# Turning matmuls that use half of TensorE's array, and moving transfers between queues, in a two-layer hybrid decoder trunk

## The chip, the cores and the metric

The kernel runs on one core of one Trainium2 chip. The metric is the device time of one execution in microseconds (us). The core has five engines that run beside each other: TensorE (PE; its weight loads are the row PEld), VectorE (DVE), ScalarE (ACT), GpSimd (POOL) and SyncE (SP), which here only issues transfers.

## The reference

Two decoder layers over 256 tokens of width 1024, all float32. Each layer projects the tokens, runs three mixers on parts of the projection, gates and sums them, and ends in a SwiGLU network. Cut to what matters here:

```python
for l in range(DEPTH):
    p = x @ w_in[l]
    y_a = rwkv7_time_mix(p[..., :o_mla], ...)      # 8 heads of 64, recurrence over the tokens
    y_b = mla_branch(p[..., o_mla:o_s5], ...)      # 8 heads, softmax(q k) v, causal
    y_c = s5_branch(p[..., o_s5:o_gate], ...)      # 32 groups, diagonal complex state space
    gates = sigmoid(p[..., o_gate:] + gate_b[l])
    merged = gates[0] * y_a + gates[1] * y_b + gates[2] * y_c
    x = layer_norm(ALPHA * x + merged @ w_out[l], ln1_g[l], ln1_b[l])
    h = silu(x @ ffn_w1[l]) * (x @ ffn_w3[l])
    x = layer_norm(ALPHA * x + h @ ffn_w2[l], ln2_g[l], ln2_b[l])
```

The RWKV step is `state = state * w + (state a) b + v k`, `y = state r`, one 64x64 state per head.

## The kernel before

**Weights.** All large weights come as 138 chunks per layer, 128x1024 float32 (0.5 MB; four of a layer have 832 columns). `w_load` (L156) issues the transfer into `raw` on SP (L160), ACT rounds it to `whi` (L161), and DVE, with POOL's help at times, forms the rest `wlo` (L171, L173). There are three `raw` buffers and four pairs `whi`/`wlo`; `w_next` keeps up to four chunks ahead. A projection (`mm3`, L206 to L208) is three matmuls per block: high by high, high by low, low by high. These projections are most of PE's work.

**Order.** The mixers are written as short pieces, and two tables of tokens, `ORDER1` and `ORDER2` (one row per layer), say in which order the pieces are issued: `S`, `m`, `r` and `G` are projections (S5 input, latents, RWKV input, gates), `P` loads the small parameters, `T` makes the S5 tables, `t` is an S5 tile, `N` the latents' norm; in the second table `p`, `s`, `i`, `v`, `n` are the RWKV pieces `prep`, `scores`, `inverse`, `solve` and `norm`, `a` and `b` the two halves of `attn`, and `l`, `o`, `h`, `f` projections of outputs and gates. A scheduler then sets each engine's order from these pieces, the pools' buffers and its own estimates. Each engine runs its list strictly in that order.

**Small products.** Many products use only part of the 128x128 array: 64 rows, or 64 columns, or a quarter. A plain float32 matmul is two passes (two records each in the profile). The ones that the change touches:
- `s5_tile` (L726): eight products with 64 rows each, four on the lower half of the partitions, then four on the upper.
- `prep` (L867, L871): the two lora products, rows 0 to 63 and 64 to 127; L921 transposes v; L891 and L916 are other transposes.
- `scores` (L940): four products of head 0 (lower rows), then four of head 1 (upper rows), into two banks.
- `solve` (L1031 to L1070): the recurrence for a pair `g` of head blocks (`e` = 0, 1, each two heads) in four steps `b` of 64 tokens. In a step, L1031 and L1035 form the right side, it is copied to `RH` (tile Gc) by ACT, L1043 multiplies by the inverse, DVE copies the result into `ST`, L1053 and L1055 form the new state, and two DVE operations (L1059) scale it into `S0`. Both head blocks lie on the same half `rb` of the partitions. At the end L1067 and L1070 form the outputs of all four steps.
- `attn` (L1217 to L1221): per call, two heads `hg` and `hg + 4`; each is transposed, copied to `PT` (two buffers) and multiplied by v. An even `hg` writes columns 0 to 63 of the array, an odd one 64 to 127, of one bank that is held from the even call to the odd one.

**Transfers besides weights.** `token_major` (L498) is the output projection and the second FFN product, with the layer norm. It loads `lg`, `lb` (0.5 MB each) and `xk` (1 MB) at the chunk `at`: 2 of 8 and 12 of 22. All on SP. `U2`, the S5 input in another layout, comes by eight small transfers (L695), also on SP. POOL makes the next layer's S5 tables beside layer 0's FFN (last operations L384 to L389) in buffers that are freed when it is done and that `lg`, `lb` and `xk` of the second product then take.

## Time and profile before

| | us |
|---|---|
| median of three runs | 1076.62 (1067.44, 1076.62, 1078.77) |
| profiled execution | 1068.97 |
| its span, first to last instruction | 1067.1 |
| PE, DVE, ACT, POOL busy | 1014.2, 784.7, 482.6, 235.2 |

The mean granted TensorE clock is 0.986 of 2.4 GHz. Busy time of PE is the union of its matmuls; a matmul's length includes the end of its pipeline, some 0.2 us in which the next one already runs. So in a timeline the distance from start to start tells what a matmul costs, not its length. The chain that ended last is 58% PE, 17% DVE, 9% POOL and 7% DMA.

### The profile page before, as it was taken

The page shows a single profiled execution, that of the slowest core. Times are in us where ns is not written, and L with a number is a line of the kernel's source. Part 1 is how long each engine was busy: PE and PEld are TensorE (multiplying, and loading weights), DVE is VectorE, ACT ScalarE, POOL GpSimd, SP SyncE. Part 2 cuts the span into 40 slices and gives each one's busy share as a digit, 9 for nine tenths or more (in the row PEclk, how much of TensorE's full clock was granted, in tenths as well). Part 3 has the DMA queues.
Part 4 walks back from the last instruction along what each step waited for, and adds up shares of the span by engine and source line. Part 5 has one row for each costly group of instructions (what it writes and reads, how often), then busy time and mean ns, then how long its engine had stood idle before and what let it go on. Part 6 is the DMA issues. An engine that isn't in the chain of part 4 may idle for free.

```text
span 1067.1 us, 21219 instructions
## 1 busy us (share of the span) xinstructions
PE 1014.2 (95%) x8560; PEld 912.5 (86%) x8560; DVE 784.7 (74%) x1542; ACT 482.6 (45%) x797; POOL 235.2 (22%) x262
## 2 busy tenths in 40 slices
PE   8799989999999999799999999999999999999997
PEld 7798778888896999798878999778889879999885
DVE  7969978976578778386474998888747876667546
ACT  5544477534244244144325346865334423443431
POOL 2970222300000599500012003221002420000000
PEclk9989999999999999999999999999999999999999
DMA  8442241223385555466536325232234755555562
GB/s 280 156 159 90 91 147 41 92 89 100 93 294 177 197 180 171 162 207 217 185 123 218 126 81 191 79 98 85 76 100 173 252 190 215 183 188 183 179 196 79
DMA packets 47394, 163.86 MB, mean 154 GB/s; under 512 B 5696, under 2 KB 8256, under 8 KB 46400
## 3 DMA queue, kind: packets, MB, share of 16 engines
q1 hardware_dynamic: 47008, 161.98, 45.9%
q8 instruction: 67, 1.10, 0.4%
q10 hardware_dynamic: 288, 0.52, 0.1%
q14 instruction: 31, 0.25, 0.1%
HBM read 156.72 MB, written 4.19 MB: 151 GB/s over the span
## 4 chain that ended last, share of the span: by engine, by line
PE 58%; DVE 17%; POOL 9%; DMA 7%; ACT 5%; issue 3%; SPq 0%; DVEq 0%; ACTq 0%; POOLq 0%
PE mm L208 11%; PE mm L207 10%; PE mm L206 10%; DMA raw<-in_ws 6%; DVE wlo L171 3%; PE mm L511 3%; PE mm L512 3%; PE mm L510 3%; ACT whi L161 3%; DVE z L745 1%; PE pa L726 1%; PE pb L1035 1%; POOL st L387 1%; PE pb L1043 1%; PE pa L940 1%
## 5 line engine op out<-in xcount | busy, mean ns | idle before, releaser
L171 DVE TENSOR_TENSOR wlo<-raw,whi 128x1024 fp32r<-128x1024 f32 (+2 forms) x265 | 333.5, 1262 | 171.8 <-ACT whi L161 169.1
L161 ACT CAST whi<-raw 128x1024 fp32r<-128x1024 f32 (+2 forms) x267 | 277.4, 1043 | 379.8 <-PE mm L207 211.8
L206 PE MATMUL mm<-xh,whi 128*128 128x256 f32 x1312 | 376.9, 287 | 14.2 <-ACT whi L161 13.9
L208 PE MATMUL mm<-xh,wlo 128*128 128x256 f32 x1312 | 376.1, 287 | 2.9 <-DVE wlo L171 2.6
L207 PE MATMUL mm<-xl,whi 128*128 128x256 f32 x1312 | 375.1, 286 | 0.4 <-DVE xl L262 0.4
L206 PEld LDWEIGHTS mm<-xh,whi 128*128 128x128 f32 x1312 | 249.2, 190 | 18.6 <-ACT whi L161 14.5
L208 PEld LDWEIGHTS mm<-xh,wlo 128*128 128x128 f32 x1312 | 250.2, 191 | 7.6 <-DVE wlo L171 4.0
L207 PEld LDWEIGHTS mm<-xl,whi 128*128 128x128 f32 x1312 | 250.2, 191 | 2.7 <-DVE xl L262 0.6
L240 POOL TENSOR_TENSOR rs<-rs,mhalf 128x1 f32<-128x1 f32 x8 | 7.8, 971 | 341.2 <-DVE rs L238 341.2
L206 PE MATMUL mm<-yh,whi 128*128 128x256 f32 x256 | 74.6, 291 | 0.1
L207 PE MATMUL mm<-yl,whi 128*128 128x256 f32 x256 | 74.1, 289 | 0.0
L208 PE MATMUL mm<-yh,wlo 128*128 128x256 f32 x256 | 74.1, 289 | 0.0
L511 PE MATMUL mm<-wlo,hh 128*128 128x512 f32 x132 | 52.0, 394 | 0.0
L510 PE MATMUL mm<-whi,hh 128*128 128x512 f32 x132 | 51.7, 394 | 0.0
L512 PE MATMUL mm<-whi,hl 128*128 128x512 f32 x132 | 51.5, 392 | 0.0
L206 PEld LDWEIGHTS mm<-yh,whi 128*128 128x128 f32 x256 | 48.5, 189 | 2.3 <-ACT qa L113 0.9
L207 PEld LDWEIGHTS mm<-yl,whi 128*128 128x128 f32 x256 | 48.5, 190 | 1.2 <-issue 0.8
L208 PEld LDWEIGHTS mm<-yh,wlo 128*128 128x128 f32 x256 | 48.6, 190 | 1.1 <-issue 0.7
L240 POOL TENSOR_TENSOR rsn<-rsn,mhalf 128x8 f32<-128x8 f32 x4 | 6.5, 1634 | 142.8 <-DVE rsn L238 142.8
L173 POOL TENSOR_TENSOR wlo<-raw,whi 128x384 fp32r<-128x384 f32 (+2 forms) x24 | 27.7, 1162 | 44.6 <-ACT whi L161 42.5
L947 POOL TENSOR_SCALAR_AFFINE_SELECT Mk<-Mk 64x512 f32<-64x512 f32 x32 | 27.0, 844 | 43.6 <-ACT Mk L113 42.3
L510 PEld LDWEIGHTS mm<-whi,hh 128*128 128x128 f32 x132 | 24.8, 188 | 6.2 <-DVE th L1284 0.8
(487 smaller groups left out, 1745.7 us busy)
## 6 DMA issues: line engine op xcount, KB each, us to landing
raw<-in_ws SPq DMA_DIRECT2D x267, 512.0 KB, 3.8
raw<-in_ws SPq DMA_DIRECT2D x8, 416.0 KB, 3.5
xd<-xk SPq DMA_DIRECT2D x3, 1024.0 KB, 4.1
xk<-xd SPq DMA_DIRECT2D x3, 1024.0 KB, 7.4
lg<-in_lnv SPq DMA_DIRECT2D x4, 512.0 KB, 5.0
lb<-in_lnv SPq DMA_DIRECT2D x4, 512.0 KB, 5.7
pc<-in_spC SPq DMA_DIRECT2D x2, 768.0 KB, 5.3
pb<-in_spB SPq DMA_DIRECT2D x2, 512.0 KB, 4.9
```

The lines of the kernel that those rows point to most:

```text
L161: S.copy(out=hi[:, s], in_=raw[:, s])
L171: V.tensor_tensor(out=lo[:, 0:m], in0=raw[:, 0:m], in1=hi[:, 0:m].bitcast(F32), op=ALU.subtract)
L173: G.tensor_tensor(out=lo[:, m:w], in0=raw[:, m:w], in1=hi[:, m:w].bitcast(F32), op=ALU.subtract)
L206: PE.matmul(ps, lhsT=wh, rhs=xh, start=first, stop=False)
L207: PE.matmul(ps, lhsT=wh, rhs=xl, start=False, stop=False)
L208: PE.matmul(ps, lhsT=wl, rhs=xh, start=False, stop=last)
L240: G.tensor_tensor(out=out, in0=in_, in1=mh(out), op=ALU.pow)
L387: E.tensor_tensor(out=s1, in0=c0, in1=ls, op=ALU.mult)
L510: PE.matmul(acc[b][n], lhsT=ah, rhs=w[0][:, s], start=(k == 0), stop=False)
L511: PE.matmul(acc[b][n], lhsT=ah, rhs=w[1][:, s], start=False, stop=False)
L512: PE.matmul(acc[b][n], lhsT=al, rhs=w[0][:, s], start=False, stop=(k == nk - 1))
L947: G.affine_select(out=Mk[r, h], in_=Mk[r, h], pattern=[[0, 4], [1, 2], [1, 64]], compare_op=ALU.is_ge, fill=0.0, base=-1, channel_multipli ...
```

## The change

- A helper `in_turn` issues matmuls in a fixed sequence. With it the S5 input products, the lora products and the scores alternate between the lower and upper row half, and take both banks at once.
- `solve` is mirrored: the head block `e` = 1 now has its time halves swapped (`rb` is a list, one slice per head block), so that in each step the two blocks lie on opposite halves. Products of both alternate. `RH` is one copy of 128x128 instead of 64x256 on ACT; `ST` is copied by ACT for `e` = 0 and DVE for `e` = 1. The output block alternates over the steps' halves.
- For that, odd blocks in `prep` write B and K in swapped places (one more DVE operation), transpose v by two-pass products into the swapped column halves, and two index expressions in `inverse` are mirrored (not shown).
- `attn` keeps `PT` of an even call (three buffers) and multiplies in the odd call, alternating the column halves; its bank is held only there.
- `U2` is loaded from ACT's queue instead of SP's.
- `token_major` issues its loads, `xk` in two halves, spread over the chunks in the list `at`, each behind the last weight transfer issued.
- In layer 1's first table `r0` moves ahead of `N t0`.

```diff
-    "m S0 S1 P N t0 r0 r1 r2 t1 r3 w0 w1 t2 t3 g0 r4 r5 w2 w3 G3 G1 G2 r6 G0 g1",
+    "m S0 S1 P r0 N t0 r1 r2 t1 r3 w0 w1 t2 t3 g0 r4 r5 w2 w3 G3 G1 G2 r6 G0 g1",
...
-            SY.dma_start(out=raw[:, s], in_=ws[i, :, s])
+            state["dma"] = SY.dma_start(out=raw[:, s], in_=ws[i, :, s])
...
+    def in_turn(mms):
...
+        last = None
+        for ps, lhsT, rhs in mms:
+            with tc.issue_after(inst(last)) if last is not None else ExitStack():
+                last = PE.matmul(ps, lhsT=lhsT, rhs=rhs, start=True, stop=True)
...
+        loads = [(xk[:, 0], x_dram[:, 0]), (lg, lnv[l, ln:ln + 1, :].to_broadcast([128, D])),
+                 (lb, lnv[l, ln + 1:ln + 2, :].to_broadcast([128, D])), (xk[:, 1], x_dram[:, 1])]
...
-            if k == at:
-                SY.dma_start(out=lg, in_=lnv[l, ln:ln + 1, :].to_broadcast([128, D]))
-                SY.dma_start(out=lb, in_=lnv[l, ln + 1:ln + 2, :].to_broadcast([128, D]))
-                SY.dma_start(out=xk, in_=x_dram)
...
+            if k in at:
...
+                with tc.issue_after(inst(state["dma"])):
+                    for o, i in loads[at.index(k)::len(at)]:
+                        SY.dma_start(out=o, in_=i)
...
-                        SY.dma_start(out=U2[r:r + 32, j // 2::2, :], in_=u[32 * j:32 * j + 32, :, i, :])
+                        S.dma_start(out=U2[r:r + 32, j // 2::2, :], in_=u[32 * j:32 * j + 32, :, i, :])
...
+                pss = [mxps("a"), mxps("a")]
+                in_turn([(pss[pp][:, 256 * qq + 128 * ri:256 * qq + 128 * ri + 128],
+                          bl[64 * pp:64 * pp + 64, 2 * F + qq, ri, :], U2[64 * pp:64 * pp + 64, 2 * F + qq, :])
+                         for qq in range(2) for ri in range(2) for pp in range(2)])
...
-                    ps = mxps("a")
-                    for qq in range(2):
-                        for ri in range(2):
-                            PE.matmul(ps[:, 256 * qq + 128 * ri:256 * qq + 128 * ri + 128],
-                                      lhsT=bl[64 * pp:64 * pp + 64, 2 * F + qq, ri, :],
-                                      rhs=U2[64 * pp:64 * pp + 64, 2 * F + qq, :], start=True, stop=True)
-                    ps4 = ps.rearrange("p (q r t) -> p q r t", q=2, r=2)
+                    ps4 = pss[pp].rearrange("p (q r t) -> p q r t", q=2, r=2)
...
-                ps = mxps("a")
-                PE.matmul(ps[:, 0:256], lhsT=w2a2[0:64, 128 * f:128 * f + 128], rhs=ld[0:64], start=True, stop=True)
+                pss = [mxps("a"), mxps("a")]
+                in_turn([(pss[i][:, 0:256], w2a2[64 * i:64 * i + 64, 128 * f:128 * f + 128], ld[64 * i:64 * i + 64])
+                         for i in range(2)])
...
-                S.activation(out=uu, in_=ps[:, 0:256], func=AF.Tanh, bias=hw0[:, f:f + 1], scale=0.5)
-                ps = mxps("a")
-                PE.matmul(ps[:, 0:256], lhsT=w2a2[64:128, 128 * f:128 * f + 128], rhs=ld[64:128], start=True, stop=True)
+                S.activation(out=uu, in_=pss[0][:, 0:256], func=AF.Tanh, bias=hw0[:, f:f + 1], scale=0.5)
...
-                S.activation(out=ta, in_=ps[:, 0:256], func=AF.Tanh, bias=ha0[:, f:f + 1], scale=0.5)
+                S.activation(out=ta, in_=pss[1][:, 0:256], func=AF.Tanh, bias=ha0[:, f:f + 1], scale=0.5)
...
-                    PE.transpose(ps[:, 128 * b:128 * b + 128], vT[:, f, 128 * b:128 * b + 128], ident)
+                    if e:
+                        for i in range(2):
+                            o = 128 * b + 64 * i
+                            PE.matmul(ps[64 - 64 * i:128 - 64 * i, 128 * b:128 * b + 128], lhsT=vT[:, f, o:o + 64], rhs=ident,
+                                      start=True, stop=True, skip_group_check=True)
+                    else:
+                        PE.transpose(ps[:, 128 * b:128 * b + 128], vT[:, f, 128 * b:128 * b + 128], ident)
...
-                    r = slice(64 * i, 64 * i + 64)
+                    r = slice(64 * (i ^ e), 64 * (i ^ e) + 64)
...
+                pss = [mxps("a"), mxps("a")]
+                in_turn([(pss[h][:, 128 * b:128 * b + 128],
+                          BK[64 * h:64 * h + 64, b // 2, 2 * (b % 2):2 * (b % 2) + 2].rearrange("p a t -> p (a t)"),
+                          AR[64 * h:64 * h + 64, :, b]) for b in range(4) for h in range(2)])
...
-                    o = slice(64 * h, 64 * h + 64)
-                    ps = mxps("a")
-                    for b in range(4):
-                        PE.matmul(ps[:, 128 * b:128 * b + 128],
-                                  lhsT=BK[o, b // 2, 2 * (b % 2):2 * (b % 2) + 2].rearrange("p a t -> p (a t)"),
-                                  rhs=AR[o, :, b], start=True, stop=True)
-                    cp(9, out=Mk[:, h].rearrange("p b a t -> p (b a t)"), in_=ps)
+                    cp(9, out=Mk[:, h].rearrange("p b a t -> p (b a t)"), in_=pss[h])
...
-                    rb, rk = slice(64 - 64 * i, 128 - 64 * i), slice(64 * i, 64 * i + 64)
+                    rb = [slice(64 * (1 - i ^ e), 64 * (1 - i ^ e) + 64) for e in range(2)]
+                    rk = rb[::-1]
...
+                    if b:
+                        for e in range(2):
+                            PE.matmul(ps[rb[e], 0:128], lhsT=ARs[e][:, 0, b, :], rhs=S0[:, e, b - 1], start=True,
+                                      stop=False, skip_group_check=True)
+                    for h in range(2):
+                        o = slice(64 * h, 64 * h + 64)
+                        for e in range(2):
+                            PE.matmul(ps[rb[e], o], lhsT=Mks[e][rk[e], h, b, 0, :], rhs=ST[rk[e], e, c2, i, h, :],
+                                      start=(b == 0), stop=True, skip_group_check=True)
+                    RH = t1("Gc", (128, 4, 65))[:, 0:2, 0:64]
+                    cp(16, out=RH, in_=v2(ps[:, 0:128], 2))
+                    ps = mxps("b")
+                    for h in range(2):
+                        for e in range(2):
+                            PE.matmul(ps[rb[e], 64 * h:64 * h + 64], lhsT=DTf[rb[e], 4 * e + 2 * h + c2, :],
+                                      rhs=RH[rb[e], h, :], start=True, stop=True, skip_group_check=True)
...
-                        if b:
-                            PE.matmul(ps[rb, 128 * e:128 * e + 128], lhsT=ARs[e][:, 0, b, :], rhs=S0[:, e, b - 1], start=True,
-                                      stop=False, skip_group_check=True)
-                        for h in range(2):
-                            o = 128 * e + 64 * h
-                            PE.matmul(ps[rb, o:o + 64], lhsT=Mks[e][rk, h, b, 0, :], rhs=ST[rk, e, c2, i, h, :],
-                                      start=(b == 0), stop=True, skip_group_check=True)
-                    RH = t1("Gc", (128, 4, 65))[:, :, 0:64]
-                    cp(16, out=RH[rb], in_=v2(ps[rb, 0:256], 4))
-                    ps = mxps("b")
-                    for e in range(2):
-                        for h in range(2):
-                            o = 128 * e + 64 * h
-                            PE.matmul(ps[rb, o:o + 64], lhsT=DTf[rb, 4 * e + 2 * h + c2, :], rhs=RH[rb, 2 * e + h, :],
-                                      start=True, stop=True, skip_group_check=True)
-                    cp(17, out=ST[rb, :, c2, i], in_=ps[rb, 0:256].rearrange("p (e h v) -> p e h v", e=2, h=2))
+                        cp(16 + e, out=ST[rb[e], e, c2, i], in_=v2(ps[rb[e], 0:128], 2))
...
-                    for b in range(4):
-                        r, o = slice(64 * (b % 2), 64 * (b % 2) + 64), 256 * (b // 2) + 128 * e
-                        if b:
-                            PE.matmul(ps[r, o:o + 128], lhsT=ARs[e][:, 1, b, :], rhs=S0[:, e, b - 1], start=True, stop=False,
-                                      skip_group_check=True)
+                    for c2 in range(2):
...
+                                r = slice(64 * (b % 2), 64 * (b % 2) + 64)
+                                PE.matmul(ps[r, o:o + 128], lhsT=ARs[e][:, 1, b, :], rhs=S0[:, e, b - 1], start=True,
+                                          stop=False, skip_group_check=True)
...
-                            PE.matmul(ps[r, o + 64 * h:o + 64 * h + 64], lhsT=Mks[e][:, h, b, 1, :],
-                                      rhs=ST[:, e, b // 2, b % 2, h, :], start=(b == 0), stop=True, skip_group_check=True)
+                            for b in bs:
+                                r = slice(64 * (b % 2), 64 * (b % 2) + 64)
+                                PE.matmul(ps[r, o + 64 * h:o + 64 * h + 64], lhsT=Mks[e][:, h, b, 1, :],
+                                          rhs=ST[:, e, c2, b % 2, h, :], start=(b == 0), stop=True, skip_group_check=True)
...
-                    acc_o[0] = mxps("c")
-                po = acc_o[0]
-                o = 64 * (hg % 2)
+                    acc_o[0] = []
+                else:
+                    po = mxps("c")
...
-                    PT = mqs[0].tile([128, 384], F32, tag="PT", name="PT", bufs=2)
+                    PT = mqs[0].tile([128, 384], F32, tag="PT", name="PT", bufs=3)
...
-                    PE.matmul(po[o:o + 64, 256 * i:256 * i + 256], lhsT=vt[:, 0, 64 * h:64 * h + 64], rhs=PT[:, 0:256],
-                              start=True, stop=False, skip_group_check=True)
-                    PE.matmul(po[o:o + 64, 256 * i + 128:256 * i + 256], lhsT=vt[:, 1, 64 * h:64 * h + 64],
-                              rhs=PT[:, 256:384], start=False, stop=True, skip_group_check=True)
-                if hg % 2 == 1:
-                    cp(26, out=yB[0][:, hg // 2::2], in_=v2(po, 2))
-                    V.tensor_tensor(out=yB[1][:, hg // 2::2], in0=v2(po, 2),
-                                    in1=yB[0][:, hg // 2::2].bitcast(F32), op=ALU.subtract)
+                    if hg % 2 == 0:
+                        acc_o[0].append((PT, h, 0))
+                        continue
...
+                    two = acc_o[0][i], (PT, h, 64)
+                    for p, h, o in two:
+                        PE.matmul(po[o:o + 64, 256 * i:256 * i + 256], lhsT=vt[:, 0, 64 * h:64 * h + 64], rhs=p[:, 0:256],
+                                  start=True, stop=False, skip_group_check=True)
+                    for p, h, o in two:
+                        PE.matmul(po[o:o + 64, 256 * i + 128:256 * i + 256], lhsT=vt[:, 1, 64 * h:64 * h + 64],
+                                  rhs=p[:, 256:384], start=False, stop=True, skip_group_check=True)
+                if hg % 2 == 0:
+                    yield
+                    return
+                cp(26, out=yB[0][:, hg // 2::2], in_=v2(po, 2))
+                V.tensor_tensor(out=yB[1][:, hg // 2::2], in0=v2(po, 2),
+                                in1=yB[0][:, hg // 2::2].bitcast(F32), op=ALU.subtract)
...
-            token_major(gate0[1], 8, 0, False, q, l, 2)
+            token_major(gate0[1], 8, 0, False, q, l, [0, 1])
...
-                token_major((hh, hl), NF, 2, l == layers - 1, q2, l, 12)
+                token_major((hh, hl), NF, 2, l == layers - 1, q2, l, [9, 10, 11, 12])
```

The scheduler's result, at three places. On PE, in layer 0's first pair, step 3 of the recurrence before (S is `S0`, Gc is `RH`, c the identity; `mm` rows are projections):

```order
L207 MATMUL mm<-xl,whi 128x256
L208 MATMUL mm<-xh,wlo 128x256
L1031 MATMUL pb<-S_1666,kr__236 64x128
L1035 MATMUL pb<-ST,Mk 64x64 x2
L1031 MATMUL pb<-S_1666,kr__236 64x128
L1035 MATMUL pb<-ST,Mk 64x64 x2
L206 MATMUL mm<-xh,whi 128x256
L207 MATMUL mm<-xl,whi 128x256
L208 MATMUL mm<-xh,wlo 128x256
L206 MATMUL mm<-xh,whi 128x256
L1043 MATMUL pb<-Gc,DTf_1662 64x64 x4
L1053 MATMUL pb<-S_1666,c 64x64
```

The same and the next step after the change, with line numbers moved by some 10 to 30:

```order
L1051 MATMUL pb<-S_1666,kr__236 64x128 x2
L1056 MATMUL pb<-ST,Mk 64x64 x4
L1063 MATMUL pb<-Gc,DTf_1662 64x64 x4
L1074 MATMUL pb<-S_1666,c 64x64
L1076 MATMUL pb<-ST,BKt 64x64
L1074 MATMUL pb<-S_1666,c 64x64
L1076 MATMUL pb<-ST,BKt 64x64
L1074 MATMUL pb<-S_1666,c 64x64
L1076 MATMUL pb<-ST,BKt 64x64
L1074 MATMUL pb<-S_1666,c 64x64
L1076 MATMUL pb<-ST,BKt 64x64
L1051 MATMUL pb<-S_1666,kr__236 64x128 x2
```

The two head blocks' L1051 and L1056 now stand as one group each, and steps 3 and 4 follow each other with no projection in between.

On SP, layer 0's FFN before, from the load of `pb` (the S5 parameters for the tables) on:

```order
L363 DMA pb<-in_spB 128x1024
L160 DMA raw<-in_ws 128x1024 x23
L516 DMA lg<-in_lnv 128x1024
L517 DMA lb<-in_lnv 128x1024
L518 DMA xk<-xd_4219 128x2048
L160 DMA raw<-in_ws 128x1024 x14
```

And after:

```order
L370 DMA pb<-in_spB 128x1024
L160 DMA raw<-in_ws 128x1024 x37
L160 DMA raw<-in_ws 128x832 x2
L160 DMA raw<-in_ws 128x1024 x10
L529 DMA xk<-xd_4234 128x1024
L160 DMA raw<-in_ws 128x1024
L529 DMA lg<-in_lnv 128x1024
L160 DMA raw<-in_ws 128x1024
L529 DMA lb<-in_lnv 128x1024
L160 DMA raw<-in_ws 128x1024
```

The three loads stood after 23 weight chunks; they are now four loads, the first behind 49, with a chunk between them.

On ACT, layer 0's start before (`bd` and `cd` are table tiles that wait for DVE, `kr` takes a projection):

```order
L161 CAST whi<-raw 128x1024
L113 COPY u<-mm 128x2x128 x2
L161 CAST whi<-raw 128x1024
L418 ACTIVATE bd<-pb,c 128x32x16
L418 ACTIVATE cd<-pb,c 128x32x16 x2
L161 CAST whi<-raw 128x1024
L418 ACTIVATE bd<-pb,c 128x32x16
L593 ACTIVATE kr__236<-mm,dv 128x256
L418 ACTIVATE bd<-pb,c 128x32x16
L593 ACTIVATE kr__236<-mm,dv 128x256
```

And after:

```order
L705 DMA U_248<-u 32x4x128 x8
L161 CAST whi<-raw 128x1024 x2
L603 ACTIVATE kr__236<-mm,dv 128x256
L425 ACTIVATE bd<-pb,c 128x32x16
L425 ACTIVATE cd<-pb,c 128x32x16 x2
L603 ACTIVATE kr__236<-mm,dv 128x256
L161 CAST whi<-raw 128x1024
L603 ACTIVATE kr__236<-mm,dv 128x256
L161 CAST whi<-raw 128x1024
L425 ACTIVATE bd<-pb,c 128x32x16
```

The eight U transfers come in behind the copies of u, and the casts of weights stand otherwise among the `bd` and `cd` writes.

## Rows read from the trace of the kernel before

**Rows 1.** The profile's first part: busy time, share of the span, instructions.
```profile
PE 1014.2 (95%) x8560; PEld 912.5 (86%) x8560; DVE 784.7 (74%) x1542; ACT 482.6 (45%) x797; POOL 235.2 (22%) x262
```

**Rows 2.** Busy us of each engine by stretch (us), PE clock, DMA share, GB/s.
```profile
45.00:70.00 25.00, 16.94 (x164) 15.96 (x163) 18.80 (x18) 14.99 (x24) 24.53 (x17) 0.77 0.37 123
100.00:125.00 25.00, 23.04 (x328) 19.85 (x330) 25.00 (x59) 10.28 (x19) 0.99 (x1) 1.00 0.13 43
444.00:455.00 11.00, 3.70 (x26) 3.20 (x25) 1.49 (x2) 2.35 (x4) 0.00 (x0) 0.83 0.87 330
455.00:475.00 20.00, 20.00 (x156) 20.00 (x157) 16.95 (x29) 9.50 (x12) 0.00 (x0) 0.92 0.68 217
600.00:650.00 50.00, 48.88 (x593) 44.21 (x592) 48.67 (x101) 20.01 (x31) 5.38 (x5) 1.00 0.32 105
820.00:870.00 50.00, 47.66 (x297) 42.43 (x295) 37.37 (x46) 21.69 (x25) 18.37 (x14) 0.97 0.73 251
```

**Rows 3.** PE timeline, first RWKV solve: start us, length us, what, passes.
```profile
216.25 0.67 PE L1035 MATMUL pb<-ST,Mk 64*64 64x64 f32 x8
216.86 0.39 PE L207 MATMUL mm<-xl,whi 128*128 128x256 f32 x1
...
219.75 0.45 PE L1055 MATMUL pb<-ST,BKt 128*64 128x64 f32 x8
220.13 0.39 PE L208 MATMUL mm<-xh,wlo 128*128 128x256 f32 x1
...
221.16 0.43 PE L1031 MATMUL pb<-S,kr__236 128*64 128x128 f32 x2
...
221.89 0.43 PE L1031 MATMUL pb<-S,kr__236 128*64 128x128 f32 x2
...
222.62 0.39 PE L206 MATMUL mm<-xh,whi 128*128 128x256 f32 x1
```

**Rows 4.** PE timeline at the lora, score and inverse products.
```profile
122.19 0.48 PE L867 MATMUL pa<-ld,pc 64*128 64x256 f32 x1
122.20 0.48 PE L871 MATMUL pa<-ld,pc 64*128 64x256 f32 x1
...
157.96 2.01 PE L940 MATMUL pa<-kr__236,BK 64*128 64x128 f32 x16
...
208.34 0.76 PE L983 MATMUL pb<-D,n 32*32 32x32 f32 x64
```

**Rows 5.** PE timeline, value products of one head group.
```profile
164.87 0.65 PE L1219 MATMUL pc<-PT,vt 128*64 128x256 f32 x2
...
165.57 0.59 PE L1219 MATMUL pc<-PT,vt 128*64 128x256 f32 x2
...
166.32 0.44 PE L891 MATMUL pa<-c,kr 128*128 128x128 f32 x2
```

**Rows 6.** SP's wait and PE's timeline near 440 us.
```profile
SPq L516 <- POOL st L389: 15.5, 1, 15.5
...
453.54 0.58 PE L206 MATMUL mm<-xh,whi 128*128 128x256 f32 x1 [6.83 <-ACT whi L161]
```

**Rows 7.** PE's wait and ACT's timeline in layer 0's start.
```profile
PE mm L206 <- ACT whi L161: 5.6, 1, 5.6
...
48.67 1.33 ACT L418 ACTIVATE cd<-pb,c 128x512 f32<-128x512 f32 x2 [4.98 <-DVE pb L408]
```

**Rows 8.** U2's transfers on SP (ns min/median/max), and PE's wait for them.
```profile
L695 SPq DMA_DIRECT2D U<-u x16: 585/600/2259, 33.4 to 582.5; - x16
...
PE pa L726 <- DMA U<-u: 2.3, 1, 2.3
```

**Rows 9.** Copies of the chain: duration ns min/median/max.
```profile
L113 ACT COPY PT<-pb x16: 472/479/498, 163.8 to 763.8; 128x384 f32<-128x384 f32 x16
...
L113 ACT COPY Gc<-pb x16: 360/367/368, 217.0 to 798.8; 64x256 f32<-64x256 f32 x16
...
L1059 DVE TENSOR_TENSOR S<-pb,gam x24: 282/289/296, 220.3 to 795.9; 64x128 f32<-64x128 f32 x24
```

More of the change, by code (lines that the diff above doesn't have):

```diff
@@ L907, in prep @@
                 b4 = be.rearrange("p (c a) t -> p c a t", c=2)
-                V.scalar_tensor_tensor(out=BK[:, :, 1:3], in0=kk.rearrange("p (c a t) -> p c a t", c=2, a=2), scalar=0.5,
-                                       in1=b4, op0=ALU.mult, op1=ALU.mult)
-                V.tensor_tensor(out=BK[:, :, 0::3], in0=kp.rearrange("p (c a t) -> p c a t", c=2, a=2), in1=b4, op=ALU.mult)
+                inner, outer = BK[:, :, 1:3], BK[:, :, 0::3]
+                k4 = kk.rearrange("p (c a t) -> p c a t", c=2, a=2)
+                if e:
+                    for i in range(2):
+                        V.scalar_tensor_tensor(out=outer[:, i], in0=k4[:, i], scalar=0.5, in1=b4[:, i], op0=ALU.mult,
+                                               op1=ALU.mult)
+                else:
+                    V.scalar_tensor_tensor(out=inner, in0=k4, scalar=0.5, in1=b4, op0=ALU.mult, op1=ALU.mult)
+                V.tensor_tensor(out=inner if e else outer, in0=kp.rearrange("p (c a t) -> p c a t", c=2, a=2), in1=b4,
+                                op=ALU.mult)
                 BKt = t1("BKt", (128, 3, 128), 4)
@@ L920, in prep @@
                 for b in range(2):
-                    PE.transpose(ps[:, 128 * b:128 * b + 128], vT[:, f, 128 * b:128 * b + 128], ident)
+                    if e:
+                        for i in range(2):
+                            o = 128 * b + 64 * i
[3 more added lines that the diff above has]
+                        PE.transpose(ps[:, 128 * b:128 * b + 128], vT[:, f, 128 * b:128 * b + 128], ident)
                 for i in range(2):
-                    r = slice(64 * i, 64 * i + 64)
+                    r = slice(64 * (i ^ e), 64 * (i ^ e) + 64)
                     cp(8, out=ST[r, :, i], in_=ps[r, 0:256].rearrange("p (c h v) -> p c h v", c=2, h=2))
@@ L1209, in attn @@
                 if hg % 2 == 0:
-                    acc_o[0] = mxps("c")
-                po = acc_o[0]
-                o = 64 * (hg % 2)
+                    acc_o[0] = []
+                else:
+                    po = mxps("c")
                 for i, h in enumerate(hs):
-                    PT = mqs[0].tile([128, 384], F32, tag="PT", name="PT", bufs=2)
+                    PT = mqs[0].tile([128, 384], F32, tag="PT", name="PT", bufs=3)
                     ps = mxps("b")
```

8 lines of the change are left out of this document (6 added, 2 removed).

## The prediction

> **What bounds the kernel now.** I read first the busy shares. TensorE is busy 95% of the span [rows 1], and VectorE, next, 74%. A busy PE is not a full PE, so the second view is the busy time stretch by stretch, and the reader should look there for stretches in which PE is well under its length. There are few [rows 2]: 16.94 of 25 us at 45 to 70, 3.70 of 11 us at 444 to 455, 47.66 of 50 us at 820 to 870. Elsewhere PE is full, and in the two state-space stretches (100 to 125 and 600 to 650) VectorE is full too, with 25.00 of 25 and 48.67 of 50 us.
>
> So two things can shorten the run: fewer PE microseconds where PE alone is full, and the removal of single waits. For the first I read PE's timeline in the recurrence [rows 3] and at small products [rows 4, 5], for the second the waits of the DMA queue and of ACT [rows 6 to 8].
>
> **What order on PE is worth.** In rows 3 the eight passes of L1035 (four 64x64 matmuls, two passes each), all on one quarter of the array, hold PE from 216.25 to 216.86, 0.61 us. The eight passes of L1055, whose outputs alternate between the column halves, hold it from 219.75 to 220.13, 0.38 us. Nothing else differs that would make them cheaper (their row count is even larger), so alternating saves 0.23 us per four matmuls. Rows 4 show the same for row halves: L867 and L871 start at 122.19 and 122.20 and run side by side, while sixteen passes of L940, eight on one half and then eight on the other, take 2.01 us to the last end.
>
> *Recurrence* (4 solves: two head pairs in each of two layers). Of each solve's steps 2 to 4, the block L1031/L1035 now takes 221.16 to 222.62, of which the first head block 0.73 (221.16 to 221.89). With both running on opposite halves the block costs about 0.75, which saves 0.70, three times. L1043 is the form of L1035 and saves 0.23, four times, and step 1 of L1035 another 0.23. The output block already alternates in runs of two and three, so I count 0.4 as an estimate. Sum 2.1 + 0.92 + 0.23 + 0.4 = 3.65 per solve, 14.6 us in all. The crossed quarters (one head block from the upper rows to the lower columns, the other the other way) are not in the trace at 64x64; the bounds are 0 (0.61 stays) and 0.23. I take 0.23, since in rows 4 the 64 passes of L983, on four diagonal quarters of 32, take 0.76 us to the last end, 0.012 each against 0.076 (0.61 / 8) in rows 3.
>
> *The rule that speaks against this.* L983 writes from four row groups into one PSUM bank, 64 passes in 0.76 us. The Trainium skill (TensorEngine Tiling (Array Packing), Restrictions and Gotchas) says that different row tiles cannot access the same PSUM bank at the same time, and the crossed quarters do just that. By that rule the 64x64 part of the recurrence would gain nothing; the trace of L983 disagrees with it where the outputs lie on different partitions. What a loss of that part would cost stands with the rivals.
>
> *Scores* (8 products): before 2.0 us where both halves stand together, and a little more where the schedule put other work between. In the new order the first matmul stands alone, because the second half's bank is not yet free, and seven follow. That is 0.4 for the lone one (two passes and the entry) and some 1.1 for the seven (half of 2.0 plus an entry of 0.1), 1.5: saves 0.45 to 0.5, eight times, less where a score shared its entry with a neighbour: 3.5 us.
>
> *Value products* (4 groups of eight matmuls): before, four of one half take 164.87 to 166.32, 1.45 us, of which 0.70 (164.87 to 165.57) is one head's [rows 5], so a group costs 2.9 and, split as it mostly stands, 3.2. Run in turn eight cost what four do, 1.45; but three of the four groups are split by the schedule into two or three visits, so I count 2.2 on average and save 1.1, four times, 4.5 us. The lora products in `prep` are split in the new order and gain nothing.
>
> *S5 input* (8 products of the form of L940): the same arithmetic would save 0.7 each, 5.5 us. But it lies where VectorE is full [rows 2], and there a PE that finishes earlier waits. Bounds 0 and 5.5; I take 1.5.
>
> *Added work:* the odd heads' transposes of v become two-pass matmuls on column halves, 0.2 to 0.6 us, four times, 1.6 us more; further entries into other tilings in the new order I put at 2 us.
>
> PE sum: 14.6 + 3.5 + 4.5 + 1.5 - 1.6 - 2 = 20.5 us.
>
> **What is late next.** The recurrence is a chain: products, copy to SBUF, products. Copies cost 367 ns (Gc on ACT) and two of 289 ns (S on DVE), PT 479 ns [rows 9]. Before, projection matmuls stood between every two links. With shorter bursts the filler runs out: in the new order the last two steps of layer 0's first pair stand back to back, five links without filler, and layer 1 has one. A bare link costs pipeline end 0.22, copy 0.37 (two copies 0.58) and restart, 0.7 to 0.9 us: 6 x 0.7 = 4.2 us given back. The last value products of each layer stand bare too, behind four PT copies through three buffers: 2 x 1.2 = 2.4 us. VectorE is nearly full in the RWKV stretches also: 1.4 us. Net PE gain 20.5 - 8 = 12.5 us. The ends are 0 (all of it waits for VectorE) and 20.5.
>
> **The waits.**
> - *The DMA queue in layer 0's first FFN product.* SP waits 15.5 us at L516, the load of `lg`, for POOL's `st` of L389, whose buffers `lg` takes over; all weight loads behind it stand still, and PE waits 6.83 us at 453.54 [rows 6]. The stretch 444 to 455 holds 3.70 us of work in 11 [rows 2], so 7.3 us idle; in the idle time the granted clock fell to its lower level, 1.2 GHz, and its mean over the 20 us behind is 0.92, which costs 1.6 more. In the new order 49 weight loads instead of 23 stand between `pb` and the first such load, which is then one of `xk` behind ffn2's own weights. That gives back 8.9. It could be less only if the weights themselves waited for POOL, for which nothing stands on the queue: 7 to 9.5.
> - *Layer 0's start.* ACT waits 4.98 us before `cd` for DVE [rows 7], a weight cast stands behind it, and PE runs dry for 5.6 us. In the new order four casts stand between the first pair of `cd` writes and the second, where one stood. Against it: the eight U2 issues now lie on ACT, 600 ns each [rows 8], 5 us in which ACT casts nothing; it frees SP of as much. Bounds -3 and +6, I take +3.
> - *Layer 1's start.* PE waits 2.3 us for U2 [rows 8]; with r0's 48 matmuls and the latents' transposes ahead, it is landed by then: +2. Cover gone it would be 0.
> - *token_major's loads* of 2 MB: in layer 1 the second set moves from the output projection, where PE loses 2.34 us of 50 with DMA at 0.73 [rows 2], into ffn2: +1.5, bounds -3 (they now meet the last weights) and +3.
>
> **Sum.** 12.5 + 8.9 + 3 + 2 + 1.5 = 27.9 us. The profiled execution took 1068.97 us (span 1067.1 and 1.9 around it): 1041. The three timed runs were 1067.44, 1076.62 and 1078.77, their median 7.7 above it; I add 3 for that: **1044 us**.
>
> **Rivals.**
> 1. *VectorE swallows PE's gain.* For it: 100% and 97% busy in the S5 stretches [rows 2]; against it: it has slack elsewhere. Then 12.5 us go and the waits stay: 1044 + 12 = 1056.
> 2. *Crossed quarters don't overlap.* L1043 (16 bursts) and the 64x64 part of L1031/L1035 (16) lose 0.23 each, 7.4: 1051. For it the rule above, against it L983.
> 3. *Fillers are plentiful and layer 0's start clears wholly:* 4 us of bare links and 6 of the start return: 1034 or somewhat less.
> 4. *Slower: the state copies queue behind weight casts on ACT.* Half of the ST copies move from DVE to ACT, so 16 ST and 16 Gc copies there meet casts of about 1 us in static order. Price: 32 copies times the delay that no filler covers. It decides from 27.9 / 32 = 0.9 us each, nearly a whole cast every time; with that and 5 us of U2 issue per layer exposed, 1044 + 28 + 10 = 1082. Against it: ACT is busy under half the time, and fillers of about 1 us remain at most links.
>
> **How the numbers follow.** Forecast 0.58, rival 1 0.17, rival 2 0.11, rival 3 0.10, rival 4 0.04. The range goes from 1028 (rival 3 and the low end of the runs) to 1062 (rival 1 plus the spread of the runs). About 1% is what a measurement of this kernel can tell from no change, so faster is below 1066: all but rival 4 and the upper tail of rival 1: 0.88, within 1% 0.08, slower 0.04.
>
> **What would show it.** Right: no PE wait near 440, SP never waiting for `st`; L1056 and L1063 in 0.4 us per four; value products in 1.45 us where they stand whole; short PE waits for the Gc and ST copies late in the first pair's solve. Wrong: PE idle spread over the RWKV stage with VectorE near 100% (rival 1), 0.6 us bursts (rival 2), ACT's copies waiting behind `whi` (rival 4), or a new long SP wait at the `xk` loads.

## The result, and the profile after

The changed kernel takes 1081.91 us (median of 11 runs, 1076.05 to 1087.47), the kernel before 1076.62 (1067.44 to 1084.0, 11 runs): a ratio of 1.0076, 95% interval 1.0047 to 1.0105. It is a little slower, where 1044 was forecast. The profiled execution has a span of 1079.2 us against 1067.1, at a mean granted clock of 0.973 against 0.986.

The first part of the page after, which answers to [rows 1]:

```profile
PE 1011.2 (94%) x8584; PEld 903.1 (84%) x8584; DVE 783.5 (73%) x1546; ACT 484.8 (45%) x813; POOL 237.6 (22%) x262
```

PE is busy 3 us less, in a span 12 us longer. The stretches of [rows 2], after (same columns):

```profile
45.00:70.00 25.00, 17.12 (x119) 16.43 (x117) 23.44 (x21) 12.72 (x19) 24.53 (x17) 0.80 0.38 126
100.00:125.00 25.00, 22.57 (x291) 19.31 (x290) 25.00 (x62) 11.06 (x24) 1.08 (x1) 1.00 0.17 57
444.00:455.00 11.00, 11.00 (x94) 11.00 (x93) 9.93 (x12) 4.88 (x6) 10.61 (x7) 1.00 0.49 151
```

The gap at 444 to 455 is gone: PE is full there, at full clock. Layer 0's start (45 to 70) is hardly better than before.

The loss shows best when the 5712 projection matmuls (the fp32r ones, the same number in every kernel here) are numbered in the order in which they start, and the time between the starts of two numbers is taken from each trace. One profiled execution each, us; the last four columns are experiments that follow:

| projections, stage | before | after | scores_back | loads_back | scores_loads_back | solve_alone |
|---|---|---|---|---|---|---|
| 0 to 420, layer 0's start | 75.9 | 77.2 | 77.0 | 76.8 | 75.8 | 71.9 |
| 420 to 1260, S5 to last solve | 209.3 | 212.9 | 206.4 | 215.0 | 206.5 | 205.0 |
| of it 700 to 1260, behind S5's last product | 143.2 | 146.1 | 138.2 | 145.3 | 138.2 | 138.9 |
| 1500 to 1680, output projection and norm | 41.6 | 48.4 | 47.6 | 41.4 | 41.5 | 41.8 |
| 2200 to 2460, FFN | 40.7 | 31.2 | 31.2 | 31.2 | 31.2 | 41.0 |
| 2880 to 3480, layer 1's start and S5 | 99.8 | 105.4 | 103.9 | 104.5 | 106.1 | 100.2 |
| 3480 to 4140, prep to last solve | 160.1 | 162.7 | 157.2 | 162.9 | 157.2 | 156.5 |
| 4320 to 4560, output projection and norm | 52.4 | 54.3 | 55.4 | 54.3 | 51.0 | 56.0 |
| all 5700 | 1049.5 | 1061.9 | 1048.4 | 1056.4 | 1039.2 | 1044.1 |

The rest differs by under 1 us between before and after. So the change won 9.5 us in the FFN and lost some 22 elsewhere. Two things stand out: both stretches with the recurrence, where PE should have been faster, became longer (2.9 behind S5 in layer 0, 2.5 in layer 1), and layer 0's output projection took 6.8 more. (Layer 1's start and S5, 5.6 more, comes up in experiments 8 and 11.) The row 700 to 1260 can be trusted to a fraction of a us: traces in which PE runs the same order there agree within 0.1 us at full clock (143.2 in before and ffn_loads_alone; 138.2 in scores_back, scores_grouped, scores_loads_back, u2_back_too and u2_split), and with half clock in it after and loads_back differ by 0.8.

**The recurrence.** PE's timeline in layer 0's first solve, after (start us, length us):

```profile
228.44 0.44 PE L1051 MATMUL pb<-S,kr__236 128*64 128x128 f32 x4
228.80 0.45 PE L1056 MATMUL pb<-ST,Mk 64*64 64x64 f32 x8
229.18 0.39 PE L214 MATMUL mm<-xl,whi 128*128 128x256 f32 x1
...
234.88 0.45 PE L1056 MATMUL pb<-ST,Mk 64*64 64x64 f32 x8
...
235.75 0.45 PE L1063 MATMUL pb<-Gc,DTf 64*64 64x64 f32 x8 [0.42 <-ACT Gc L113]
...
238.10 0.44 PE L1051 MATMUL pb<-S,kr__236 128*64 128x128 f32 x4 [0.77 <-DVE S L1080]
238.47 0.45 PE L1056 MATMUL pb<-ST,Mk 64*64 64x64 f32 x8
...
239.62 0.69 PE L1063 MATMUL pb<-Gc,DTf 64*64 64x64 f32 x8 [0.70 <-ACT Gc L113]
```

At 228.44 all is as counted: the right side of both head blocks in 0.74 us (228.44 to 229.18; before 1.46, [rows 3]), the eight quarter passes in 0.38 (228.80 to 229.18; before 0.61). The crossed quarters do run side by side. But from 234.5 on no projection stands between the links. PE waits at each one, and at 239.62 the same eight passes have become longer. The windows show why (busy us of PE, PEld, DVE, ACT, POOL, then the granted clock, DMA share, GB/s):

```profile
235.00:240.00 5.00, 3.00 (x52) 2.24 (x52) 4.23 (x19) 0.93 (x4) 0.00 (x0) 0.89 0.35 122
240.00:245.00 5.00, 4.75 (x53) 4.11 (x51) 2.51 (x14) 0.47 (x2) 0.00 (x0) 0.50 0.00 0
245.00:250.00 5.00, 4.42 (x19) 2.69 (x19) 2.43 (x10) 2.12 (x5) 1.63 (x1) 0.59 0.00 0
250.00:255.00 5.00, 3.81 (x19) 3.22 (x20) 4.15 (x17) 2.16 (x6) 0.00 (x1) 0.75 0.01 3
```

PE was idle 2 us of 5, and then the clock fell to 0.50 of full speed, 1.2 GHz, and stayed there for most of the next 10 us, through the output block and the bare value products. PE then looks busy (4.75 of 5 us) because its work takes longer. Layer 1 shows the same behind its first solve (750 to 767 us), which has 47 projections of its own instead of 73 (the clock is 0.50 until 785):

```profile
770.00:775.00 5.00, 2.43 (x21) 2.21 (x19) 3.36 (x12) 2.83 (x5) 1.64 (x1) 0.98 0.32 107
775.00:780.00 5.00, 3.80 (x11) 2.63 (x11) 3.81 (x14) 0.00 (x0) 0.00 (x0) 0.50 0.33 105
```

**The output projection of layer 0.** SP's queue before (first fence) and after (second):

```profile
293.71 0.33 SPq L516 DMA_DIRECT2D lg<-in_lnv  x1
...
296.65 0.43 SPq L517 DMA_DIRECT2D lb<-in_lnv  x1
...
299.13 0.43 SPq L518 DMA_DIRECT2D xk<-in_xtok  x1
```

```profile
327.62 0.42 SPq L529 DMA_DIRECT2D xk<-in_xtok  x1
328.10 0.42 SPq L529 DMA_DIRECT2D lb<-in_lnv  x1
...
329.35 0.44 SPq L529 DMA_DIRECT2D lg<-in_lnv  x1
329.83 0.43 SPq L529 DMA_DIRECT2D xk<-in_xtok  x1
```

Before, the scheduler had pulled these loads 20 to 26 us ahead of the projection's first matmul (319.3 us). After (first matmul at 325.3), they are tied behind a weight transfer of the projection itself, and its last weights come behind 2 MB more. ACT's waits from 320 to 352 us after, and from 315 to 347 before (us in total, times, longest):

```profile
ACT whi L161 <- DMA raw<-in_ws: 16.7, 9, 4.2
```

```profile
ACT whi L161 <- DMA raw<-in_ws: 7.3, 6, 1.7
```

PE's longest wait from 320 to 370 after:

```profile
PE pa L497 <- DVE xk L490: 3.0, 1, 3.0
```

ACT waits 16.7 us for weights, where before it was 7.3. In DVE's timeline the layer norm's first step (L476) comes at 347.81, 3.5 us before the projection's last matmul ends; before (L469 at 337.91) it came 7.0 us ahead of that. So the norm's chain is no longer hidden, PE waits 3.0 us at L497, and half clock follows (PEclk 0.50 in 355 to 360).

### The profile page after: what moved, and what is told of

It reads as the page before. It is cut to its first block, busy times and chain, and to the rows that moved or that the text cites. A ratio compares the mean times of both kernels' runs of the same rounds, so it can differ in the third digit from the quotient of the medians.

```text
span 1079.2 us, 21305 instructions
## 1 busy us (share of the span) xinstructions
PE 1011.2 (94%) x8584; PEld 903.1 (84%) x8584; DVE 783.5 (73%) x1546; ACT 484.8 (45%) x813; POOL 237.6 (22%) x262
## 4 chain that ended last, share of the span: by engine, by line
PE 49%; DVE 9%; DMA 3%; ACT 3%; issue 2%; POOL 1%; ACTq 0%; DVEq 0%; POOLq 0%; SPq 0%
PE mm L213 10%; PE mm L215 10%; PE mm L214 10%; PE mm L518 3%; DMA raw<-in_ws 3%; PE mm L519 3%; PE mm L517 3%; ACT whi L161 1%; DVE wlo L171 1%; DVE z L753 1%; PE pc L518 1%; PE pc L517 1%; PE pc L519 1%; PE pa L209 1%; PE mm L1329 1%
## 5 line engine op out<-in xcount | busy, mean ns | idle before, releaser
L517 PE MATMUL mm<-whi,hh 128*128 128x512 f32 x132 | 51.6, 394 | 0.0
L173 POOL TENSOR_TENSOR wlo<-raw,whi 128x384 fp32r<-128x384 f32 (+2 forms) x24 | 30.8, 1290 | 50.8 <-ACT whi L161 50.8
L966 POOL TENSOR_SCALAR_AFFINE_SELECT Mk<-Mk 64x512 f32<-64x512 f32 x32 | 24.6, 768 | 61.4 <-ACT Mk L113 59.9
L518 PEld LDWEIGHTS mm<-wlo,hh 128*128 128x128 f32 x132 | 24.8, 188 | 6.0 <-DVE wlo L171 0.6
```

The lines of the kernel that those rows point to most:

```text
L173: G.tensor_tensor(out=lo[:, m:w], in0=raw[:, m:w], in1=hi[:, m:w].bitcast(F32), op=ALU.subtract)
L517: PE.matmul(acc[b][n], lhsT=ah, rhs=w[0][:, s], start=(k == 0), stop=False)
L518: PE.matmul(acc[b][n], lhsT=ah, rhs=w[1][:, s], start=False, stop=False)
L966: G.affine_select(out=Mk[r, h], in_=Mk[r, h], pattern=[[0, 4], [1, 2], [1, 64]], compare_op=ALU.is_ge, fill=0.0, base=-1, channel_multipli ...
```

## The experiments

In the diffs, - is the changed kernel unless the kernel before is named. The medians of the kernel before in the four groups of runs were 1072.1, 1075.2, 1077.4 and 1071.7.

**1. The scores as before.**

```diff
-                in_turn([... for b in range(4) for h in range(2)])
+                    for b in range(4):
+                        PE.matmul(ps[:, 128 * b:128 * b + 128], ...
```

> The changed kernel with the scores issued as in the kernel before (head 0's four products, then head 1's, each with its own bank); all else as changed. Theory 1 (the scores in turn take projections away from the recurrence: the first solve of layer 0 then begins after 1013 projection matmuls instead of 970, and has 46 instead of 64 among its own, so that it runs bare and the clock falls): with the scores back there are 969 before and 72 within, no bare link, no half clock in either solve; the two solves give back about 12 and 9 us, the scores cost 3.6 more on PE, so about 1064 us. Rival (the mirrored solve itself runs out of filler, as its bursts are shorter): the half clock stays and the scores cost 3.6 more, about 1085. Rival (the scheduler's order is luck, anything moves it): a change of either sign, and the half clock at other places.

Measured: 1070.14, ratio to the kernel before 0.998 (0.9954 to 1.0006). One edit undone, which had been counted as a gain of 3.5 us, makes the kernel 1% faster. The direction is that of theory 1, the size 10 to 12 us instead of 17. In layer 1 (3480 to 4140) both kernels run the same 1612 matmul records in another order: 157.2 us here, 162.7 in the changed kernel. The clock at the end of layer 0's first solve (219.6 to 239.2 us here) and behind it is full:

```profile
235.00:240.00 5.00, 5.00 (x80) 4.35 (x79) 4.34 (x16) 1.65 (x4) 0.00 (x0) 1.00 0.37 140
240.00:245.00 5.00, 4.90 (x36) 3.31 (x34) 3.23 (x15) 2.38 (x5) 1.64 (x1) 1.00 0.02 9
245.00:250.00 5.00, 4.76 (x40) 4.14 (x41) 4.83 (x15) 3.40 (x7) 0.00 (x0) 1.00 0.02 3
```

**2. The scores in turn alone, on the kernel before.**

```diff
-                        PE.matmul(ps[:, 128 * b:128 * b + 128], ...
+                in_turn([... for b in range(4) for h in range(2)])
```

> The kernel before with the scores in turn as its only change. PE's work falls by some 3 to 6 us. Theory 1 (scores in turn take the filler from layer 0's first solve): the first solve begins after 1013 projection matmuls with 46 of its own, a stretch of 10 us without projections follows, the clock falls there for some 10 us: about 1084, slower than before by about 8. Rival (the filler runs out only where the mirrored solve's bursts are short as well): 3 to 6 faster than before, 1072.

Measured: 1082.87, ratio 1.0104 (1.005 to 1.0158). This alone is slower than the kernel before, by about as much as the whole change (the intervals overlap). The first solve begins after 1013 projections and keeps 46, and the clock falls in it too:

```profile
230.00:235.00 5.00, 3.12 (x36) 2.25 (x35) 3.67 (x14) 0.55 (x2) 0.00 (x0) 0.97 0.33 117
235.00:240.00 5.00, 4.49 (x43) 3.74 (x43) 3.10 (x17) 0.36 (x1) 0.00 (x0) 0.50 0.02 5
```

From projection 700 to 1260 it runs the same 1478 matmul records as the kernel before, in another order: 151.4 us instead of 143.2. So the order alone costs 8 us there, and the mirrored solve is not needed for the loss.

**3. The recurrence as before, all else changed.**

```diff
-                    rb = [slice(64 * (1 - i ^ e), 64 * (1 - i ^ e) + 64) for e in range(2)]
+                    rb, rk = slice(64 - 64 * i, 128 - 64 * i), slice(64 * i, 64 * i + 64)
...
```

> The changed kernel with the recurrence as before (both head blocks on the same half, no turns in its products, v transposed and B, K placed as before); scores, value products, transfers as changed. Theory 1 (scores in turn): the first solve still begins after 1013 projection matmuls with 46 of its own, a stretch of 9 us without projections stands behind it, and layer 0's half clock stays; layer 1's first solve has 66 instead of 47 and its 9 us come back; the solves cost 10 more on PE: 1082, no change. Rival (the mirrored solve drains the filler): both half clocks go, 21 back, 10 more on PE: 1071.

Measured: 1100.34, ratio 1.0246 (1.0191 to 1.03). The first solve still begins after 1013 projections and keeps 46, so my rival, that the mirrored solve drains the filler, falls. Neither sum was right: layer 0's stretch from 700 to 1260 grew to 151.4 us (146.1 after), and layer 1's to 172.0 (162.7 after) instead of giving back 9. So in the order that the scores bring, the mirrored recurrence saves more (5.3 and 9.3) than alone (experiment 10).

**4. The scores with both banks and a fixed sequence, but head by head.**

```diff
-                          ...) for b in range(4) for h in range(2)])
+                          ...) for h in range(2) for b in range(4)])
```

> The changed kernel with the scores still taking both banks at once and still in a fixed sequence, but head 0's four products and then head 1's. Theory A (it is the alternation in a fixed sequence that moves the projections ahead of the solve; in the order, the first solve now has 72 projections instead of 46): as scores_back, 1070. Theory B (holding both banks at once stalls the pieces around it, whatever the sequence): the loss stays, 1082 or, as the scores also cost 3 more on PE, 1085.

Measured: 1068.2, ratio 0.9956 (0.992 to 0.9992). Theory A: it is the alternation. Every engine runs the very order of scores_back in this trace. Why the scheduler answers the alternation by putting 44 more projections ahead of the solve was not tried; its estimates are not in a trace. A kernel whose scores alternate while the filler stays in the solve was not built either, so what the turn itself is worth is open.

**5. The bare links filled.**

```diff
+                        for j in range(2):
+                            with tc.issue_after(inst(mm)):
+                                mm = PE.matmul(ps[:, 256 + 128 * j:384 + 128 * j], lhsT=ones, rhs=ones, ...
```

> The changed kernel with two extra 128x128 products of ones, into unused columns, behind each of the products of layer 0's first solve in steps 3 and 4 (five links, ten products that nobody reads, 2.2 us of PE work; the order of this solve is otherwise the same). Theory (the idle in the bare links makes the clock fall, and the fall, not the idle itself, is most of the loss): no half clock between 235 and 257 us, 5 to 7 us less over layer 0's solves, about 1077 in all. Rival (the small products behind it, at 240 to 252, pull the clock down by themselves): half clock as before, 0 to 2 us more. Rival (the idle itself is the loss): no change, since the dummies only fill it.

Measured: 1083.8, ratio 1.009 (1.0059 to 1.0121), no gain on 1.0076. The windows over the two last steps and what follows:

```profile
236.00:241.00 5.00, 3.86 (x46) 3.00 (x44) 3.86 (x17) 0.79 (x3) 0.00 (x0) 1.00 0.41 136
241.00:246.00 5.00, 4.17 (x70) 3.58 (x71) 3.71 (x21) 0.53 (x2) 0.00 (x0) 1.00 0.00 2
246.00:251.00 5.00, 3.77 (x32) 2.30 (x30) 4.04 (x16) 2.44 (x5) 0.90 (x1) 1.00 0.01 3
251.00:256.00 5.00, 3.87 (x27) 3.08 (x28) 2.92 (x9) 2.05 (x5) 0.73 (x1) 1.00 0.00 0
```

The mechanism holds: with less idle in the links the clock stays at 1.00, and the small products behind it do not pull it down. The size does not: 420 to 1260 takes 212.6 us instead of 212.9 (700 to 1260 144.3 instead of 146.1, but from 256 us on PE's order differs too: the second solve keeps 64 projections instead of 80). Each link became longer, as PE's timeline shows (start to start 1.50 us here, 0.87 in the changed kernel at 234.88):

```profile
236.01 0.45 PE L1064 MATMUL pb<-ST,Mk 64*64 64x64 f32 x8
236.39 0.71 PE L1048 MATMUL pb<-ones 128*128 128x128 f32 x4
237.51 0.45 PE L1072 MATMUL pb<-Gc,DTf 64*64 64x64 f32 x8 [0.41 <-ACT Gc L113]
```

The copy to `Gc` started later, and PE still waits 0.41 for it. From the first product of step 3 to the output block the changed kernel takes 5.7 us and this one 8.7, 2.9 more. What the clock is worth can be read behind that, from the output block's first product to the first projection, in the changed kernel (first fence) and here (second):

```profile
240.24 0.47 PE L1091 MATMUL pb<-S,kr__236 128*64 128x128 f32 x1
...
251.70 0.38 PE L213 MATMUL mm<-yh,whi 128*128 128x256 f32 x1 [0.68 <-ACT yh L113]
```

```profile
244.31 0.32 PE L1102 MATMUL pb<-S,kr__236 128*64 128x128 f32 x1
...
252.43 0.39 PE L213 MATMUL mm<-yh,whi 128*128 128x256 f32 x1 [0.68 <-ACT yh L113]
```

That is 11.5 us at mostly half clock and 8.1 at full clock, and the 16 projections that follow take 4.1 and 3.0. So the clock cost 4.4 us of the 7.9 that scores_back gains from 700 to 1260. The other 3.5 were not measured apart; the idle links are the likely cause.

**6. The output projection's loads as before.**

```diff
-            token_major(gate0[1], 8, 0, False, q, l, [0, 1])
+            token_major(gate0[1], 8, 0, False, q, l, 2)
```

> The changed kernel with the loads of lg, lb and xk for the output projection issued as before (all at its third chunk, not tied behind a weight transfer); those for the second FFN product stay as changed. Theory (tied behind the weights they meet the last weights of the output projection, which come late, so that the four accumulators end together and the layer norm is bare): 5 to 6 us come back in layer 0 between 320 and 360 us and 2 to 3 in layer 1: 1074. Rival (the lateness comes from the work ahead of it, not from the loads): within 2 us of the changed kernel, 1082.

Measured: 1071.96, ratio 0.9993 (0.996 to 1.0026), some 9 us less than the changed kernel: the loads cost that. Layer 0's projection goes from 48.4 to 41.4 us (table), which is 7.0 of it, layer 1's stays at 54.3, a miss of the 2 to 3 expected there. Where the other 2 us lie is not shown.

**7. Both put back.**

> The changed kernel with both put back: the scores, and the loads of the output projection. Theory (two separate losses): the gains add, 11 us and 10 us against the changed kernel's 1081.9: about 1060, some 12 below the kernel before. Rival (the lateness in layer 0's output projection is only handed on by the solve's, or the other way): little more than the better one alone, about 1069.

Measured: 1059.07, ratio 0.9856 (0.9799 to 0.9913). The two add up as expected.

**8. U2 and r0.**

> As scores_loads_back, and U2 from SP again, r0 behind N and t0 in layer 1. Theory (U2 on ACT's queue is what makes layer 1's start 4 us longer and its S5 3 us longer than in the kernel before): 4 to 6 us less than scores_loads_back. Rival (these come with the order of the stage, in scores_alone layer 1's start is longer still with U2 on SP): within 2 us of scores_loads_back, or slower.

Measured: 1056.9, ratio 0.984 (0.9784 to 0.9897): not told apart from 0.9856.

> As scores_loads_back, with U2 from ACT's queue in layer 0 and from SP in layer 1, and layer 1's r0 behind N and t0 again. Theory (U2 on ACT saves layer 0's start and S5 together 2.6 us by the two traces, 181.6 against 184.2 us, and costs layer 1's 6.8): about 3 us less than u2_back_too, 1054. Rival (these are the chance of one order): within 1 us of u2_back_too, 1057.

Measured: 1057.08, ratio 0.9808 (0.9783 to 0.9832). Also not told apart. Layer 1's start and S5 took 99.4 and 99.2 us in these two traces against 106.1 in scores_loads_back, but 106.6 in ffn_loads_alone (below), where U2 is as before. Split at projection 3200, the varying part is the start. From 3200 to 3480, S5, all eight traces with layer 1's U2 on SP and `r0` in its old place take 47.8 to 48.1 us, and all seven with U2 on ACT and `r0` moved 49.9 to 51.6. So these two edits together cost 1.7 to 3.5 us there; which of them does it was not tried, and the times do not tell it.

**9. The value products.**

> The kernel before with the value products in turn as its only change. My count was 4.5 us of PE time; no bare links come with it in the order: about 1068. Rival (VectorE or the copies of PT set the pace where they stand): no change, 1072. Rival (holding the even heads' PT in three buffers makes the last group wait): slower by 1 to 3.

Measured: 1077.45, ratio 1.0006 (0.997 to 1.0042): no gain.

> As u2_split, with the value products as in the kernel before. Theory (they save the PE time I counted): 4.5 us more than u2_split, 1058. Rival (as values_alone showed no gain, theirs is eaten where the groups stand): the same as u2_split within 1 us, or faster.

Measured: 1057.95, ratio 0.9812 (0.9785 to 0.9839), u2_split 0.9808: no difference either way in the time. In the traces, turning them saves 0.9 us from 700 to 1260 and 2.2 from 3480 to 4320 in u2_split against values_back_too, and costs 0.2 and 2.2 in values_alone against before. In the order, values_alone leaves layer 1's first solve 54 projections instead of 73, and its stretch takes 162.5 us (160.1 before); that this is the same mechanism as with the scores was not tried by itself.

**10. The mirrored recurrence alone, on the kernel before.**

> The kernel before with the mirrored recurrence as its only change (solve, and what prep and inverse need for it). Theory (turns on the array are worth what I counted, as long as the filler stays; in the order the first solve begins after 969 projections with 72 of its own, and no link is bare): 14.6 less the 1.6 for the transposes of v, some 10 to 13 us: about 1063. Rival (the recurrence is a chain of copies, shorter bursts only wait longer): within 3 us of the kernel before, 1073.

Measured: 1069.31, ratio 0.9942 (0.9911 to 0.9972), some 6 us; in the table 4.3 in layer 0 and 3.6 in layer 1. Of the rest 1.6 went into PE's wait for the group norm behind the second solves, which was in the kernel before (first line) and is here (second):

```profile
PE pc L1094 <- DVE yT L1089: 3.1, 2, 1.7
PE pc L1115 <- DVE yT L1110: 4.7, 2, 3.1
```

**11. The loads of the second FFN product alone, on the kernel before.**

> The kernel before with the loads of lg, lb and xk for the second FFN product moved as changed (output projection's as before). PE's order is the same as before. Theory (SP's wait for POOL alone causes the gap near 450): 9 us gone there and kept to the end: about 1065. Rival (given back where the loads now fall, at the end of the product, or at layer 1's start): no change, 1074.

Measured: 1064.61, ratio 0.9875 (0.9849 to 0.9902), 9.5 us at the place itself (table: 40.7; 31.2 in this trace too), and kept to the end. The whole gain is larger, 10 to 16 us by the interval, and the rest is not placed: in the trace layer 0's start is 5.0 shorter and layer 1's start and S5 6.8 longer than in before, though every engine's order is that of before but for the moved loads.

The fastest versions are u2_back_too, u2_split and values_back_too, all 1.6 to 1.9% faster than the kernel before, and not told apart among themselves. That is what experiments 10 and 11 give added up (0.6 and 1.25%); no other edit shows a gain in the time.

## Why the prediction was wrong, step by step

- **The step that failed** is *Scores*, "saves 0.45 to 0.5, eight times [...]: 3.5 us". The burst was counted right: in the trace of the changed kernel two passes and the entry take 0.42, then fourteen 1.09, 1.5 together.

```profile
160.06 0.48 PE L209 MATMUL pa<-kr__236,BK 64*128 64x128 f32 x2
160.48 0.39 PE L214 MATMUL mm<-yl,whi 128*128 128x256 f32 x1
...
161.38 1.16 PE L209 MATMUL pa<-kr__236,BK 64*128 64x128 f32 x14
162.47 0.39 PE L214 MATMUL mm<-yl,whi 128*128 128x256 f32 x1
```

What was not counted is what the edit does to the order around it: the first solve begins after 1013 projections instead of 970 and keeps 46 instead of 64. The net was a loss of 1% (experiments 1, 2, 4), and the traces place it in the two recurrence stretches: 7.9 us in layer 0 (146.1 against 138.2) and 5.5 in layer 1 (162.7 against 157.2).
- **What is late next.** The bare links were there to be read, and I did read them in the order, but put them down to shorter bursts, as a price of turning the recurrence. Experiment 3 shows that they belong to the scores. I priced them as idle alone, 0.7 us each. They also cost the clock, and everything behind them until it rose again, 4.4 us in layer 0 (experiment 5).
- **token_major's loads.** The term +1.5 looked at layer 1 only, and there the projection became 1.9 longer (52.4 to 54.3). In layer 0 the tie cost 6.8 us, and experiment 6 gives it back. "Bounds -3" was too narrow.
- **The FFN's wait** (8.9) was right: 9.5 at the place, kept to the end (experiment 11), by the mechanism named: SP no longer waits for `st`.
- **The recurrence** (14.6): per burst right, crossed quarters included, so the Trainium skill's rule on row tiles and PSUM banks (TensorEngine Tiling (Array Packing), Restrictions and Gotchas) is not borne out for outputs on different partitions (eight passes in 0.38 us). Of its 13 us (14.6 less 1.6 for the transposes) 7.9 show at the place (experiment 10), 1.6 of them went into the wait for yT, and the 5 that are missing were not traced.
- **Value products** (4.5): nothing arrived in the time, and the traces show either sign (experiment 9). **Layer 0's start** (3): 75.9 against 77.2, but ffn_loads_alone, whose order there is that of before on every engine, took 70.8, so this stage varies by more than the term. **Layer 1's start and S5** (2 and 1.5): 5.6 longer in the profile. The start varies by more than the term (99.8 for both in before, 106.6 in ffn_loads_alone); S5 lost 1.7 to 3.5 with U2 and `r0` moved and gained nothing from its input products in turn (48.1 in u2_split, 47.8 in before).
- **Rival 1** (VectorE swallows the gain) is not what happened: in the bare solve DVE was busy 2.43 to 4.23 us of 5. **Rival 4**, the slower one, named copies that queue behind casts; the `Gc` copies waited for PE's products, not for a cast. The range missed because no rival had the order itself as a cost: the bare links that the turned scores bring, and the tied loads.

With the two faulty parts out, scores_loads_back stands 1.4% under the kernel before, against the 3% forecast. Those two parts are some 23 of the 38 us between 1081.91 and 1044. The other 15 lie among the recurrence, the value products and the two starts, in shares that the runs do not settle.

## What to carry to other kernels

Where a scheduler orders the engines, price an edit by the order that comes out, not by its own instructions: count the filler that each serial chain keeps, before and after, and find which edit moved it by building with that edit alone. A serial chain that runs bare costs its links and then the clock of what follows. A load that "may come early" should not be tied behind the transfers of the stage that needs it; ties are for loads that come too early, as in the FFN here.

## What the runs showed of the hardware

- TensorE fell to half clock after 2 us idle of 5 (235 to 240 us), and kept it through a stretch that the busy share calls full (4.75 of 5 us). None of the idle pieces there was longer than 0.8 us. With the five links filled it stayed at full clock. A busy share near 95% can so hide a loss: read the granted clock beside it.
- 64x64 products on crossed quarters, eight passes in 0.38 us, run as fast as products on column halves [rows 3].
- Some stages differ by 5 to 7 us between executions though the order is the same (layer 0's start 70.8 and 75.9, layer 1's start and S5 99.8 and 106.6), so a single pair of profiles does not settle a term of 3 us there. Others repeat to 0.1 us (700 to 1260), and there it does.
